# A decoder trunk on one core: two HGRN2 units' values and gates projected in one pass of 512 columns

## The chip, the cores and the metric

The kernel runs on one core of a Trainium2 chip. The core has a matrix engine (TensorE, PE in the profile; its weight loads are listed apart as PEld), a vector engine (VectorE, DVE), a scalar engine (ScalarE, ACT), a general engine (GpSimd, POOL) and a queue engine that issues transfers (SyncE, SP). They run side by side, each in its own order, and wait for one another by semaphores. TensorE writes its results into PSUM, here eight banks of 512 floats for each of 128 partitions; the other data stand in SBUF. The metric is device time in microseconds; less is better.

## The reference

One layer of a hybrid decoder for 2048 tokens of width 1024: a token mixer and a gated MLP, each behind a normalised, conditioned input and added to the residual.

```python
def token_mixer(h, w_in, w_gla_up, b_gla, lb, head_gain, w_out, pos):
    proj = h @ w_in
    (rq, rk, rv, rg, hq, hf, hi, hg, aq, ak, av, ag, alow) = jnp.split(proj, offs, axis=-1)
    ...
    z = split_heads(hf, HG_HEADS).astype(jnp.float32)
    log_f = jnp.logaddexp(jnp.log1p(-lbh) + jax.nn.log_sigmoid(z), jnp.log(lbh))
    key_h = (1.0 - lbh) * jax.nn.sigmoid(-z)
    o_h = gated_state_chunkwise(jax.nn.silu(split_heads(hq, HG_HEADS)), key_h,
                                split_heads(hi, HG_HEADS), log_f)
    o_h = merge_heads(rms_norm(o_h)) * jax.nn.silu(hg)
    ...
    o = jnp.concatenate([o_r, o_h.astype(o_r.dtype), o_a.astype(o_r.dtype)], axis=-1) * head_gain
    return o @ w_out
```

Three kinds of heads share the input projection: retention heads (r), HGRN2 heads (h) and gated linear attention heads (a). For the HGRN2 heads `hf` gives the forget gate and the key, `hq` the query, `hi` the values and `hg` the output gate, which acts as `hg * sigmoid(hg)` (a swish) on the normalised result.

## The kernel before

**Blocks and units.** The 2048 tokens are worked on in four blocks of 512 (`b` = 0 to 3), each in four chunks of 128. Within a block the mixer's heads form units of two heads each, 128 columns: four HGRN2 units `h0` to `h3`, one unit `g` that holds the two pairs of GLA heads, and two retention units `r0`, `r1`. The list `ORDER` runs them as h0, g, h1, h2, h3, r0, r1. After the mixer the MLP runs over all tokens from about 1274 us on; the change does not touch it.

**Precision.** Each product of float32 data is made of three matmuls (`split3`, L239): every operand is split into a rounded high part and the rest as low part, and high x high, high x low and low x high are added in PSUM. A weight piece comes as raw data by DMA, ScalarE casts the high part, VectorE subtracts to get the low part (`piece`, L217; in `tf512` L293 and L299), and the low part is stored in DRAM (`keep`), so that the later blocks load it instead.

**Projections.** `cf_gemm` (L251) gives one unit's f or q with channels on the partitions: 8 x 3 matmuls of 512 tokens. `tf_gemm` (L263) gives one unit's values and gates with tokens on the partitions: for each of 8 slices of the model width and each of four chunks three matmuls, the activations being the stationary operand and 256 weight columns (128 of values, 128 of gates) the moving one; two chunks share a bank. `tf512` (L281) does the same for two such pieces of 256 columns at once, one bank for each chunk, in four quarters of weights; before the change it is used for the two pairs of g and for the retention units (q, k beside v, g).

**Emptying the banks.** `tok_evac` (L517) after `tf_gemm` and `tok_evac4` (L526) after `tf512` bring values and gates to SBUF: ScalarE copies the values, ScalarE takes the sigmoid of the gates, VectorE multiplies that sigmoid with the gates, all three reading PSUM. `tok_evac4` does one unit's four banks, then the other's. Four banks (`acc_ps`) serve all large products in turn; two more are for the level steps (`lev_ps`) and two for the rest of the chains (`late_ps`).

**Chains.** A unit's recurrence (`gated`, L586; `retention`, L799) is a generator: some matmuls, then a pause in which VectorE and ScalarE work on them, and so on. A gated chain has seven level steps (L610 on TensorE; L618, L620, L629 on VectorE), then a transpose of the keys, the state update `u` (the first to read the values `v`), the output, and after a further pause the transposed result `oT`, which reads the gates.

**The order of TensorE's work is fixed when the program is built**, by a planner (`Clock`, L55). Every group of large matmuls advances a clock by its estimated time, and chain steps are issued into the stream when their pauses are over; `clock.until` issues what is due next until a condition holds. One chain runs at a time; the others stand in line. ScalarE, VectorE and the queues are put in order by the framework, by program order and given priorities.

**Around the units.** `out_half` (L908) is the output projection of a block, in two halves of four units: the first at the block's end, the second (`out_finish`, L927) in the next block behind h0, since it needs the last chains' results. It adds into the residual rows `x1`, which stand in four "xy" buffers, and forms the second norm; when the rows are done with (`then`, L935), the buffers come free. The same buffers serve `weight_sums` (L873), 22 small jobs that form sums of MLP weights on VectorE in blocks 1 to 3, and `early_sums` in block 3. `ada_next` brings in one row of the conditioning weights with each weight piece while any are queued, 16 of them in block 1; such a row uses one of the two raw weight buffers.

Of the kernel before, what the change touches and what calls it, by code (L numbers as in the profile page):

```python
# [9 lines left out]
F32 = mybir.dt.float32  # L10
# [3 lines left out]
AF = mybir.ActivationFunctionType  # L14
ALU = mybir.AluOpType
# [85 lines left out]
def trunk(ctx, tc, xT, vecs, cvec, cst, rope, msk, wada, win, walow, wgla, wout, wup, wdown, out):  # L101
# [24 lines left out]
    def late_ps(name):  # L126
        return pp.tile([P, 512], F32, tag="late", name=name, bufs=2)
# [152 lines left out]

    def tf512(name, i):  # L281

        pss = [acc_ps(f"ps{name}_{c}") for c in range(NCH)]
        for q4 in range(4):
            half, sub = q4 // 2, q4 % 2
            src = win[i + half:i + half + 3:2][:, :, sub * 512:(sub + 1) * 512].rearrange("a p n -> p a n")
            ada_next()
# [224 lines left out]
    def tok_tiles(name):  # L512

        return (pu.tile([P, NCH, P], F32, tag="v", name="v" + name, bufs=3),
                pu.tile([P, NCH, P], F32, tag="sg", name="sg" + name, bufs=3))

    def tok_evac(vsg, pss):  # L517
        v, sg = vsg
        for j, ps in enumerate(pss):
            p3 = ps[:].rearrange("p (c n) -> p c n", n=256)  # L520
            c2 = slice(2 * j, 2 * j + 2)
            S.copy(v[:, c2, :], p3[:, :, 0:P])
            S.activation(sg[:, c2, :], p3[:, :, P:256], AF.Sigmoid)
            V.tensor_tensor(sg[:, c2, :], sg[:, c2, :], p3[:, :, P:256], op=ALU.mult)

    def tok_evac4(vsg, pss, at):  # L526

        v, sg = vsg
        for c, ps in enumerate(pss):
            gate = ps[:, at + P:at + 256]  # L530
            S.copy(v[:, c, :], ps[:, at:at + P])
            S.activation(sg[:, c, :], gate, AF.Sigmoid)
            V.tensor_tensor(sg[:, c, :], sg[:, c, :], gate, op=ALU.mult)

# [51 lines left out]
    def gated(name, b, ui, pos, kq, decay, subs, qk, sel):  # L586
# [16 lines left out]
        for li, s in enumerate(LEVELS):  # L603
            nb = 64 // s
            pss = []
            for q, rows, v, sg in subs:
                ps = lev_ps(f"lv{name}_{s}")
                for c in range(NCH):
                    rhs = q[:, :, c * P:(c + 1) * P].rearrange("p h (n t s) -> p h n t s", t=2, s=s)[:, :, :, 1, :]
                    T.matmul(ps[:, c * P:(c + 1) * P].rearrange("p (h n s) -> p h n s", h=2, s=s),  # L610
                             kq[:, c * P:(c + 1) * P], rhs, start=True, stop=True)
                pss.append(ps)
            with tc.high_priority(offset=CHAIN):
                ev = tree[li]
                nn = TB // (2 * s)
                for q, rows, v, sg in subs:
                    qv = q[:].rearrange("p h (n t s) -> p h n t s", t=2, s=s)[:, :, :, 1, :]
                    V.tensor_tensor(qv, qv, ev[:, :, 0:1].unsqueeze(1).to_broadcast([P, 2, nn, s]), op=ALU.mult)  # L618
# [11 lines left out]
            adv(4 * len(subs) * MF)  # L630
            yield LEVEL_GAP[two]
        ps = late_ps("kT" + name)
        for c in range(NCH):
            T.transpose(ps[:, c * P:(c + 1) * P], kq[:, c * P:(c + 1) * P], ident)
        kT = pu.tile([P, NCH, P], F32, tag="kT", name="kT" + name, bufs=1)
        with tc.high_priority(offset=CHAIN):
            S.copy(kT[:].rearrange("p c n -> p (c n)"), ps[:])
            for q, rows, v, sg in subs:
# [4 lines left out]
        for q, rows, v, sg in subs:  # L643
            ps = late_ps("u" + name)
# [15 lines left out]
        os = []  # L660
        for i, ((q, rows, v, sg), at) in enumerate(zip(subs, attns)):
            if i:
# [20 lines left out]

    def unit_h(b, u, pos):
        nm = f"h{b}_{u}"
# [22 lines left out]
        clock.chain(gated(nm, b, u, pos, kq, decay, subs, qk, selh), 9.0 if b == u == 0 else 6.0)  # L708
        tok_evac(subs[0][2:], tf_gemm("vg" + nm, 4 * u + 2))

# [11 lines left out]
    def unit_g(b, pos):  # L722
# [38 lines left out]
        pss = tf512(f"vg{nm}", 18)  # L761
        for i in range(2):
            tok_evac4(subs[i][2:], pss, 256 * i)

    rots = {}

    def unit_r(b, r, pos):
# [11 lines left out]
        for c, ps in enumerate(pss):  # L779
            S.copy(a[0][:, c * P:(c + 1) * P], ps[:, 0:P])  # L780
            S.copy(a[1][:, c * P:(c + 1) * P], ps[:, P:256])
        tok_evac4(vsg, pss, 256)
        s4 = sin.unsqueeze(2).to_broadcast([P, NCH, 2, 32])
# [15 lines left out]
    def retention(nm, b, r, pos, a, kk, kc, q, vsg):  # L799
        v, sg = vsg  # L800
        Sst = states[5 + r]
# [226 lines left out]

    oTs = [[None] * KD for _ in range(NB)]
    mk = {"h": unit_h, "g": lambda b, u, pos: unit_g(b, pos), "r": unit_r}  # L1030
    PE, DVE, ACT, SP = (getattr(mybir.EngineType, n) for n in ("PE", "DVE", "Activation", "SP"))
    ctx.enter_context(tc.manual_schedule(engines={PE}))
# [3 lines left out]
    gla_weights()  # L1036
    for hi, lo, raw, i in W0.values():
        keep(f"i{i}l", lo[:])
    jobs = [job for k in range(NF // 2) for job in (("d", k), ("u", 2 * k + 1))]
    for b in range(NB):  # L1040
        pos = 0
# [522 lines left out]
```

## Time and profile before

| what | value |
|---|---|
| median of three runs | 2562.22 us |
| runs | 2557.1, 2562.22, 2563.71 us |
| the profiled execution's span | 2557.2 us |
| first matmul of the mixer's unit g in block 0 | 59.1 us |
| ends of the first output halves of blocks 0, 1, 2, 3 | 305.6, 617.1, 920.4, 1227.4 us |
| matmuls `psvgh<-hvgh,ha` etc. of 128x256 (values and gates of h units) | 1440 |
| matmuls `psqkvgr` and `psvgg` of 128x512 | 768 and 384 |

The device time of a run is about the span, so nothing noteworthy lies around it. In the profile a group of instructions is named by its line, engine, operation and out<-in, with buffer numbers and block numbers left out: `psvgh` is the bank of an h unit's values and gates, `psvgg` that of g, `pshfh` the bank of an h unit's f, `sgg` the gates of g in SBUF, `lvgh` the low part of a weight piece. Busy time of TensorE counts overlapping matmuls, so that its share says little; idle time and the distance between starts say more.

### The profile page before, as it was taken

Reading aid. Unit: us, or ns where it says so; the run is one execution under the profiler, and the core shown is the slowest. Engines: PE = TensorE matmul, PEld = TensorE weight load, DVE = VectorE, ACT = ScalarE, POOL = GpSimd, SP = SyncE. Lnnn points to the kernel's source line nnn. Section 1 sums busy time; section 2 is a strip of 40 time slices with the busy share of each in tenths; the row PEclk is TensorE's granted clock in tenths of the full one; section 3 lists DMA queues with packets and bytes.
Section 4 is the critical chain, followed back from the end, with each engine's and each line's share of the span. In section 5 each row is a group of like instructions: output and inputs, shape, how many; then the busy total and the mean of one; then the engine's idle time right before and its main releaser. Section 6 shows DMA issues by size and latency. Waiting matters only on the chain.

```text
span 2557.2 us, 37116 instructions
## 1 busy us (share of the span) xinstructions
PE 2493.1 (97%) x13146; PEld 2132.7 (83%) x13146; DVE 1973.8 (77%) x3596; ACT 1139.0 (45%) x1914; POOL 169.6 (7%) x303
## 2 busy tenths in 40 slices
PE   5999999999999999999899999999999999999998
PEld 4898888988889898898788888888878888888887
DVE  8788986878678776787688888887677778778666
ACT  4433434524444235333254555455444555455442
POOL 1000000000000000000200000000001001000000
PEclk9999999999999999999999999999999999999999
DMA  8454576775687847786745444477675544447663
GB/s 304 166 190 165 197 250 214 250 251 196 220 309 278 291 147 242 267 308 223 278 168 174 153 146 163 149 274 244 210 228 168 155 146 145 154 136 251 221 193 127
DMA packets 229337, 533.84 MB, mean 209 GB/s; under 512 B 25216, under 2 KB 28320, under 8 KB 229152
## 3 DMA queue, kind: packets, MB, share of 16 engines
q1 hardware_dynamic: 224672, 516.80, 59.5%
q0 software_dynamic: 4480, 14.68, 1.6%
q8 instruction: 103, 1.69, 0.3%
q14 instruction: 82, 0.67, 0.1%
HBM read 397.69 MB, written 133.69 MB: 208 GB/s over the span
## 4 chain that ended last, share of the span: by engine, by line
PE 78%; issue 9%; DVE 5%; DMA 4%; ACT 1%; SPq 0%; POOL 0%; DVEq 0%; ACTq 0%; POOLq 0%
PE X L241 6%; PE X L242 6%; PE X L243 6%; PE Z L241 3%; PE Z L242 3%; PE Z L243 3%; PE lvh L610 3%; PE y L241 2%; PE y L243 2%; PE y L242 2%; PE psqkvgr L243 2%; PE psqkvgr L241 2%; PE psqkvgr L242 2%; PE psvgh L242 2%; PE psvgh L241 2%
## 5 line engine op out<-in xcount | busy, mean ns | idle before, releaser
L241 PE MATMUL X<-B,A 128*128 128x512 f32 x572 | 223.5, 391 | 1.4 <-ACT u L1247 1.4
L242 PE MATMUL X<-B,A 128*128 128x512 f32 x572 | 222.9, 390 | 0.0
L243 PE MATMUL X<-B,A 128*128 128x512 f32 x572 | 222.9, 390 | 0.0
L974 DVE TENSOR_TENSOR dA<-rd,dA 128x512 fp32r<-128x512 f32 x154 | 106.1, 690 | 86.7 <-ACT dA L973 86.4
L973 ACT CAST dA<-rd 128x512 fp32r<-128x512 f32 x154 | 95.6, 621 | 139.9 <-PE dX L243 45.8
L974 DVE TENSOR_TENSOR A<-s,A 128x512 fp32r<-128x512 f32 x176 | 120.8, 686 | 43.7 <-ACT A L973 43.3
L973 ACT CAST A<-s 128x512 fp32r<-128x512 f32 x176 | 108.7, 618 | 71.5 <-PE Z L243 45.2
L241 PE MATMUL psvgh<-hvgh,ha 128*128 128x256 f32 x480 | 140.0, 292 | 0.0
L241 PE MATMUL dX<-dB,dA 128*128 128x512 f32 x352 | 137.1, 390 | 0.0
L243 PE MATMUL dX<-dB,dA 128*128 128x512 f32 x352 | 137.1, 390 | 0.0
L242 PE MATMUL dX<-dB,dA 128*128 128x512 f32 x352 | 137.1, 390 | 0.0
L242 PE MATMUL psvgh<-lvgh,ha 128*128 128x256 f32 x480 | 135.9, 283 | 1.1 <-DVE lvgh L233 1.1
L243 PE MATMUL psvgh<-hvgh,ha 128*128 128x256 f32 x480 | 135.9, 283 | 0.0
L241 PEld LDWEIGHTS X<-B,A 128*128 128x128 f32 x572 | 107.5, 188 | 24.3 <-ACT u L1247 2.2
L243 PEld LDWEIGHTS X<-B,A 128*128 128x128 f32 x572 | 107.5, 188 | 22.1
L242 PEld LDWEIGHTS X<-B,A 128*128 128x128 f32 x572 | 107.5, 188 | 22.1
L610 PEld LDWEIGHTS lvh<-qbh,kh 128*128 128x128 f32 x896 | 115.2, 191 | 8.8 <-issue 1.0
L610 PE MATMUL lvh<-qbh,kh 128*128 128x128 f32 x896 | 120.1, 277 | 1.1 <-DVE kh L620 1.0
L241 PE MATMUL Z<-B,A 128*128 128x512 f32 x308 | 120.6, 392 | 0.0
L242 PE MATMUL Z<-B,A 128*128 128x512 f32 x308 | 120.5, 391 | 0.0
L243 PE MATMUL Z<-B,A 128*128 128x512 f32 x308 | 120.4, 391 | 0.0
L974 DVE TENSOR_TENSOR dB<-rb,dB 128x512 fp32r<-128x512 f32 x154 | 105.7, 687 | 13.2 <-ACT dB L973 13.1
(463 smaller groups left out, 7129.8 us busy)
## 6 DMA issues: line engine op xcount, KB each, us to landing
gs<-yv SPq DMA_DIRECT2D x154, 256.0 KB, 2.8
rb<-gs SPq DMA_DIRECT2D x154, 256.0 KB, 4.0
r<-wup SPq DMA_DIRECT2D x141, 256.0 KB, 3.3
s<-sumsu SPq DMA_DIRECT2D x132, 256.0 KB, 3.0
wada<-wada SPq DMA_DIRECT2D x48, 512.0 KB, 5.1
rd<-sumsd SPq DMA_DIRECT2D x88, 256.0 KB, 3.8
rd<-wdown SPq DMA_DIRECT2D x66, 256.0 KB, 3.8
x<-xT SPq DMA_DIRECT2D x64, 256.0 KB, 5.6
```

What stands on the lines that cost most here:

```text
L241: T.matmul(ps, lhs[0], rhs[0], start=first, stop=False, skip_group_check=more)
L242: T.matmul(ps, lhs[0], rhs[1], start=False, stop=False, skip_group_check=more)
L243: T.matmul(ps, lhs[1], rhs[0], start=False, stop=last, skip_group_check=more)
L610: T.matmul(ps[:, c * P:(c + 1) * P].rearrange("p (h n s) -> p h n s", h=2, s=s), kq[:, c * P:(c + 1) * P], rhs, start=True, stop=True)
L973: S.copy(hi, src)
L974: V.tensor_tensor(lo, src, hi, op=ALU.subtract)
```

## The change

Two HGRN2 units' values and gates are now projected by one `tf512` pass, in place of one `tf_gemm` each. `tf512` gets a step, so that it can take the weight pieces of units 2k and 2k+1, which lie four apart. The first unit of a pair only makes its f and q and hands its tiles on; the second makes its own f and q and then the pass for both. This is done for units 2 and 3 of block 0 and for all units of blocks 1 to 3; units 0 and 1 of block 0 stay single.

Values and gates of a unit now share one tile of 256 columns per chunk. A bank is emptied by one copy per unit (128x256 each in a wide pass, 128x512 after `tf_gemm`), bank after bank and both units in each; the sigmoid and the product of the gates are done afterwards from SBUF, over all four chunks in one instruction each. A unit counts as landed when these instructions have been issued, and a gated chain waits in the planner before its transpose of the keys until its unit has landed.

In blocks 1 to 3 the units run as h0, h1, g, h2, h3, r0, r1, and the second half of the previous block's output projection follows h1 in place of h0. The low parts of units 0's values and gates, made at the start, are no longer stored.

```diff
-    def tf512(name, i):
+    def tf512(name, i, step=2):
...
-            src = win[i + half:i + half + 3:2][:, :, sub * 512:(sub + 1) * 512].rearrange("a p n -> p a n")
+            src = win[i + half:i + half + step + 1:step][:, :, sub * 512:(sub + 1) * 512].rearrange("a p n -> p a n")
...
     def tok_tiles(name):
 
-        return (pu.tile([P, NCH, P], F32, tag="v", name="v" + name, bufs=3),
-                pu.tile([P, NCH, P], F32, tag="sg", name="sg" + name, bufs=3))
-
-    def tok_evac(vsg, pss):
-        v, sg = vsg
+        t = pu.tile([P, NCH, 256], F32, tag="v", name="v" + name, bufs=3)
+        return t[:, :, 0:P], t[:, :, P:256], (t, name)
+
+    landed = set()
+
+    def swish(name, sg):
+
+        t = tmp("sw" + name)[:].rearrange("p (c n) -> p c n", n=P)
+        S.activation(t, sg, AF.Sigmoid)
+        V.tensor_tensor(sg, sg, t, op=ALU.mult)
+
+    def tok_evac(name, vsg, pss):
+        v, sg, both = vsg
         for j, ps in enumerate(pss):
-            p3 = ps[:].rearrange("p (c n) -> p c n", n=256)
-            c2 = slice(2 * j, 2 * j + 2)
-            S.copy(v[:, c2, :], p3[:, :, 0:P])
-            S.activation(sg[:, c2, :], p3[:, :, P:256], AF.Sigmoid)
-            V.tensor_tensor(sg[:, c2, :], sg[:, c2, :], p3[:, :, P:256], op=ALU.mult)
-
-    def tok_evac4(vsg, pss, at):
-
-        v, sg = vsg
+            S.copy(both[0][:, 2 * j:2 * j + 2, :], ps[:].rearrange("p (c n) -> p c n", n=256))
+        swish(name, sg)
+        landed.add(both[1])
+
+    def tok_evac4(name, units, pss):
+
         for c, ps in enumerate(pss):
-            gate = ps[:, at + P:at + 256]
-            S.copy(v[:, c, :], ps[:, at:at + P])
-            S.activation(sg[:, c, :], gate, AF.Sigmoid)
-            V.tensor_tensor(sg[:, c, :], sg[:, c, :], gate, op=ALU.mult)
+            for at, (v, sg, both) in units:
+                S.copy(both[0][:, c, :], ps[:, at:at + 256])
+        for at, (v, sg, both) in units:
+            swish(f"{name}{at}", sg)
+            landed.add(both[1])
...
+        while any(sub[-1][1] not in landed for sub in subs):
+            yield 1.5
         ps = late_ps("kT" + name)
...
-    def unit_h(b, u, pos):
+    def unit_h(b, u, pos, then=None):
...
-        tok_evac(subs[0][2:], tf_gemm("vg" + nm, 4 * u + 2))
+        if then is None:
+            tok_evac(nm, subs[0][2:], tf_gemm("vg" + nm, 4 * u + 2))
+            return
+        other = then(subs[0][2:])
+        if other is not None:
+            tok_evac4(nm, [(0, other), (256, subs[0][2:])], tf512("vg" + nm, 4 * u - 2, 4))
...
-        for i in range(2):
-            tok_evac4(subs[i][2:], pss, 256 * i)
+        tok_evac4(nm, [(256 * i, subs[i][2:]) for i in range(2)], pss)
...
-        tok_evac4(vsg, pss, 256)
+        tok_evac4(nm, [(256, vsg)], pss)
...
+    held = []
+
+    def first_of_two(vsg):
+        held.append(vsg)
+
+    def second_of_two(vsg):
+        return held.pop()
...
-    for hi, lo, raw, i in W0.values():
+    for hi, lo, raw, i in (W0["f"], W0["q"]):
         keep(f"i{i}l", lo[:])
...
-        for i, (kind, u) in enumerate(ORDER):
+        for i in range(len(ORDER)) if b == 0 else (0, 2, 1, 3, 4, 5, 6):
+            kind, u = ORDER[i]
+            pos = i + (i > 1)
             if i == len(ORDER) - 3 and b + 1 < NB:
                 norm1_stat(b + 1)
-            mk[kind](b, u, pos)
-            pos += 2 if kind == "g" else 1
+            if kind == "h" and (b or u > 1):
+                unit_h(b, u, pos, second_of_two if u % 2 else first_of_two)
+            else:
+                mk[kind](b, u, pos)
...
-            if i == 0 and b:
+            if i == 2 and b:
                 clock.until(lambda: None not in oTs[b - 1])
                 out_finish(b - 1)
```

More of the change, by code (lines that the diff above doesn't have):

```diff
@@ L605, in gated @@
             pss = []
-            for q, rows, v, sg in subs:
+            for q, rows, v, sg, _ in subs:
                 ps = lev_ps(f"lv{name}_{s}")
@@ L615, in gated @@
                 nn = TB // (2 * s)
-                for q, rows, v, sg in subs:
+                for q, rows, v, sg, _ in subs:
                     qv = q[:].rearrange("p h (n t s) -> p h n t s", t=2, s=s)[:, :, :, 1, :]
@@ L637, in gated @@
             S.copy(kT[:].rearrange("p c n -> p (c n)"), ps[:])
-            for q, rows, v, sg in subs:
+            for q, rows, v, sg, _ in subs:
                 r0, r1 = rows[1]
@@ L642, in gated @@
         yield 1.8
-        for q, rows, v, sg in subs:
+        for q, rows, v, sg, _ in subs:
             ps = late_ps("u" + name)
@@ L660, in gated @@
         os = []
-        for i, ((q, rows, v, sg), at) in enumerate(zip(subs, attns)):
+        for i, ((q, rows, v, sg, _), at) in enumerate(zip(subs, attns)):
             if i:
@@ L799, in retention @@
     def retention(nm, b, r, pos, a, kk, kc, q, vsg):
-        v, sg = vsg
+        v, sg, _ = vsg
         Sst = states[5 + r]
@@ L1040, in trunk @@
     for b in range(NB):
-        pos = 0
         if b == 2:
             later += range(40, 48)
-        for i, (kind, u) in enumerate(ORDER):
+        for i in range(len(ORDER)) if b == 0 else (0, 2, 1, 3, 4, 5, 6):
+            kind, u = ORDER[i]
+            pos = i + (i > 1)
             if i == len(ORDER) - 3 and b + 1 < NB:
                 norm1_stat(b + 1)
-            mk[kind](b, u, pos)
-            pos += 2 if kind == "g" else 1
+            if kind == "h" and (b or u > 1):
+                unit_h(b, u, pos, second_of_two if u % 2 else first_of_two)
+            else:
+                mk[kind](b, u, pos)
             if b == 0 and i == 2:
```

## The prediction

> **What bounds the kernel now.** I read the page first, then the table of stages, then TensorE's waits, then single stretches of the timeline.
>
> ```profile
> span 2557.2 us, 37116 instructions
> PE 2493.1 (97%) x13146; PEld 2132.7 (83%) x13146; DVE 1973.8 (77%) x3596; ACT 1139.0 (45%) x1914; POOL 169.6 (7%) x303
> PE 78%; issue 9%; DVE 5%; DMA 4%; ACT 1%; SPq 0%; POOL 0%; DVEq 0%; ACTq 0%; POOLq 0%
> ```
>
> ```profile
> 59.00:305.00 246.00, 243.83 (x1516) 215.44 (x1517) 201.82 (x448) 98.55 (x191) 9.61 (x17) 1.00 0.53 185
> 305.00:617.00 312.00, 309.01 (x1921) 274.07 (x1920) 245.89 (x576) 129.92 (x235) 17.51 (x30) 1.00 0.66 227
> 617.00:920.00 303.00, 301.44 (x1871) 267.12 (x1870) 236.39 (x551) 120.04 (x221) 15.78 (x26) 1.00 0.75 261
> 920.00:1227.00 307.00, 302.37 (x1856) 267.52 (x1855) 224.36 (x511) 120.01 (x227) 18.24 (x30) 0.99 0.69 244
> 1227.00:1274.00 47.00, 37.82 (x181) 31.06 (x180) 27.42 (x52) 13.66 (x25) 11.91 (x25) 0.96 0.83 303
> ```
>
> The first four stages are the mixer's blocks 0 to 3 (columns: length, then busy time of PE, PEld, DVE, ACT, POOL, then clock, DMA share, GB/s). TensorE is idle for 1.6 to 4.6 us in each: a block lasts as long as its matmuls take to issue, plus a few stalls. VectorE, at 73 to 82%, is the second engine. All work of the change lies before 1227 us. The waits of TensorE name the stalls:
>
> ```profile
> PE ssn L319 <- DVE san L340: 6.0, 1, 6.0
> PE pshfh L241 <- ACT sgg L532: 4.1, 1, 4.1
> PE psvgh L242 <- DVE lvgh L233: 1.1, 1, 1.1
> ```
>
> So the change can win in two ways, cheaper issue of the same products or a stall removed, and lose in one, a new stall.
>
> **Cheaper issue.** A matmul's duration in the trace overlaps the next one's, so the price of one is the distance of starts.
>
> ```profile
> 325.68 0.28 PE L241 MATMUL psvgh<-hvgh,ha 128*128 128x256 f32 x1
> ...
> 332.03 0.28 PE L243 MATMUL psvgh<-hvgh,ha 128*128 128x256 f32 x1
> ...
> 1018.79 0.39 PE L242 MATMUL psvgg<-lvgg,ha 128*128 128x512 f32 x1
> ...
> 1020.38 0.39 PE L243 MATMUL psvgg<-hvgg,ha 128*128 128x512 f32 x1
> ```
>
> The first pair of rows are the 1st and 54th matmul of an unbroken stretch of 256 columns: 6.35/53 = 0.1198 us each. The second pair are the 1st and 8th of a stretch of 512 columns, of just the form that the new passes have: 1.59/7 = 0.2271. One unit's values and gates are 8 slices x 4 chunks x 3 = 96 matmuls of 256 columns. A pair of units costs 192 x 0.1198 = 23.0 us now and 96 x 0.2271 = 21.8 after: **1.2 us less per pair**. There are 7 pairs (units 2 and 3 of block 0; both pairs of blocks 1 to 3): **-8.4 us**. Nothing lies beside this on TensorE, it is the path itself. Bounds: -7.4 (0.120 against 0.229, as in passes that are often broken by level steps) to -10.
>
> The Trainium skill (TensorE: Matmul & The Clock Gate, "Wait — 56ns, not 53.3ns?") puts the cost that a warm matmul has beyond its columns at about 2.5 ns; the rows put it at 2 x 119.8 - 227.1 = 12.5 ns. By the page, 7 x 96 x 2.5 ns is an estimated 1.7 us instead of 8.4: it is taken up as a rival.
>
> **The emptying of banks.** Now L522 to L524 and L531 to L533 read each bank three times, the last time on VectorE; after, ScalarE copies and the rest works in SBUF.
>
> ```profile
> L522 ACT COPY vh<-psvgh 128x256 f32<-128x256 f32 x32 | 11.9, 373 | 50.2 <-PE psvgh L243 50.1
> L523 ACT ACTIVATE sgh<-psvgh 128x256 f32<-128x256 f32 x32 | 12.5, 393 | 0.1
> L524 DVE TENSOR_TENSOR sgh<-sgh,psvgh 128x256 f32<-128x256 f32 x32 | 13.3, 417 | 10.1 <-ACT sgh L523 9.8
> L691 ACT ACTIVATE sfh<-pshfh 128x512 f32<-128x512 f32 x15 | 8.8, 588 | 1.4 <-PE pshfh L243 1.4
> L703 DVE TENSOR_TENSOR sqh<-sqh,fh 128x512 f32<-128x512 f32 x16 | 11.0, 688 | 0.1
> ```
>
> Two units cost ScalarE 4 x (0.373 + 0.393) = 3.1 us now, and 8 x 0.373 + 2 x 0.588 = 4.2 after; VectorE 4 x 0.417 = 1.7 now, 2 x 0.688 = 1.4 after. With ScalarE under 45% busy the extra microsecond is hidden. What matters is when a bank comes free: two copies, 0.75 us, against the 6 x 0.227 = 1.36 us that TensorE spends on a bank in the pass's last quarter. So ScalarE follows bank by bank, and only if it is held for over 4 us (three banks' work) does the next product wait. I take 0, bounds 0 and +1 per block.
>
> For the gated unit g the order of release matters today: unit 0's gates of all four banks are worked off before unit 1's first copy, so bank 0 comes free after the last. In block 3 this went wrong:
>
> ```profile
> 1024.27 0.40 PE L243 MATMUL psvgg<-hvgg,ha 128*128 128x512 f32 x1
> 1028.73 0.77 PE L241 MATMUL pshfh<-ha,hhfh 128*128 128x512 f32 x1 [4.05 <-ACT sgg L532]
> ...
> 1033.98 0.54 PE L241 MATMUL pshfh<-ha,hhfh 128*128 128x512 f32 x1
> 1028.22 0.27 ACT L531 COPY vg<-psvgg 128x128 f32<-128x128 f32 x1 [2.13 <-DVE sgg L533]
> 1025.05 2.43 DVE L629 COPY_PREDICATED atg<-m_all,lvg 128x512 f32<-128x512 uint32 x2
> ```
>
> TensorE idled 4.05 us because ScalarE's copy waited for VectorE's gate product in the same bank, which stood behind 2.43 us of level masks. The stall costs more than its length: the next twelve matmuls start (1033.98 - 1028.73)/12 = 0.4375 us apart, at about half speed, 12 x 0.21 = 2.5 us more. From 1024.27 the first full-speed start would be 0.23 later, so the whole is 4.2 + 2.5 = **6.7 us**. After, no VectorE instruction reads these banks and both units leave bank 0 first. I take -6.7; bounds -6.7 and 0 (ScalarE itself may be late).
>
> **The extra low parts.** Units 0 and 1 of block 0 keep the old weight layout, so block 1 has no stored low parts for its first pair: four subtractions on VectorE and four stores in place of four loads. Block 0 makes as many as before. Two stores of units 0's low parts go. Raw loads stay four per pair.
>
> ```profile
> L299 DVE TENSOR_TENSOR lqkvgr<-rqkvgr,hqkvgr 128x1024 fp32r<-128x1024 f32 x8 | 9.8, 1225 | 3.8 <-ACT hqkvgr L293 3.8
> L197 DVE CUSTOM_DVE_ANT_0 wada<-wada,c_act,vec 128x1024 f32<-128x1024 f32 x32 | 40.9, 1281 | 9.7 <-DMA wada<-wada 8.7 <-issue 0.8
> 320.00:330.00 10.00, 10.00 (x77) 9.48 (x76) 9.68 (x24) 2.76 (x4) 1.60 (x3) 1.00 0.51 191
> 330.00:340.00 10.00, 10.00 (x88) 10.00 (x87) 9.55 (x21) 3.79 (x7) 0.00 (x0) 1.00 0.78 279
> 340.00:350.00 10.00, 10.00 (x56) 8.60 (x55) 9.38 (x15) 3.91 (x6) 0.00 (x0) 1.00 0.66 231
> ```
>
> 4 x 1.225 = 4.9 us fall where VectorE is 94 to 97% busy, and in the same passes each piece also brings a conditioning row (1.28 us), which shares the two raw buffers. Hidden if that stretch has slack, all exposed if not: +2 taken, bounds 0 and +5 (plus 2.5 of slow clock should one wait pass 4 us).
>
> **The order.** In blocks 1 to 3 unit 1 moves ahead of g, and the last half of the previous block's output projection now stands behind units 0 and 1 instead of behind unit 0: 48 matmuls of f and q and 96 wide ones come before it, 96 narrow ones leave: 48 x 0.227 + 21.8 - 11.5 = 21 us, with the level steps that fall inside about 24. Unit 0's chain waits in the planner until its values land, but it gives its 7 level steps during unit 1's products, which last longer; TensorE is not empty meanwhile: 0, with +1 as bound. Queued behind the late projection are its rows x1. They hold all four "xy" buffers, for which the weight sums of block 2 wait, and for those the next x1 rows:
>
> ```profile
> 690.15 0.33 SPq L877 DMA_DIRECT2D wsd<-wdown  x1
> 868.40 0.69 DVE L884 TENSOR_TENSOR wsu<-wsu,wsu 128x512 f32<-128x512 f32 x1
> 863.64 0.38 SPq L916 DMA_DIRECT2D x<-xT  x1
> 877.56 0.85 SPq L916 DMA_DIRECT2D x<-xT  x2
> DMA to landing us min/median/max: 3.5/6.3/7.5
> 887.65 0.75 DVE L920 SCALAR_TENSOR_TENSOR x<-y,mod,x 128x512 f32<-128x512 f32 x1
> 901.62 0.74 DVE L920 SCALAR_TENSOR_TENSOR x<-y,mod,x 128x512 f32<-128x512 f32 x1
> ```
>
> The 12 jobs run back to back from 690 to 869, and the rows are issued at 864 to 878 for a use at 888. Shifted by 24 the first row lands at 864 + 6 + 24 = 894 and is used at about 888 - 5 = 883 (the block's own gain): 11 us late. But four banks stand between: the fifth row block takes the first bank only near 902 - 5 = 897. So the slack falls to about 3 us. I take +1, bounds 0 and +8 here; the price beyond that is the slower rival.
>
> At the mixer's end the order brings the last chain some microseconds earlier against the products, so the stretch 1227 to 1274 may lose a little of its idle 9 us: -1 taken, bounds -8 and +4.
>
> **Sum:** -8.4 - 6.7 + 2 + 1 - 1 = -13.1 on a profiled 2557.2, hence 2544. That execution lies at the low end of the runs shown (2557.1 to 2563.7, the span fills it), 5.0 under their median, so the median goes to 2562.2 - 13.1 = **2549**.
>
> **Rivals.** A measurement of this kernel can tell 0.3%, 7.7 us, from no change.
>
> (a) *Only the narrow saving.* ScalarE is held itself when g's banks are full (casts of the sums made early, masks, weight casts), or a like stall comes elsewhere: -8.4 + 2 + 1 - 1 = -6.4, 2556. For it: the stall came once in four blocks, so it hangs on chance order; against: the released instruction waited for VectorE, which is out of the way.
>
> (b) *The fixed cost is 2.5 ns:* 7 x 96 x 2.5 ns = 1.7 in place of 8.4, so -6.4 again, 2556. The rows of both widths speak against it. This is the page's rule, named above.
>
> (c) *VectorE becomes the bound in block 1:* two quarters of the new pass each wait over 4 us at 6.7 a time: -13.1 - 2 + 13.4 = -1.7, 2560. For it 94 to 97%; against: TensorE has no idle time there now.
>
> (d) *The x1 rows come too late, slower.* Place: end of block 2. If each of the 12 jobs also takes 2 us longer, rows come 24 us later still, 21 beyond the cover, and the slow clock adds 2.5: -13.1 - 1 + 23.5 = +9.4, 2572. It decides from a slip of about 3 us beyond the 24. For it: the chain of jobs has no gaps; against: the same work, no more bytes, and in block 3 the rows are in time by over 20 us.
>
> (e) *The end of the mixer tightens too:* its 8 us go: -13.1 - 7 = -20, 2542.
>
> **Chances.** Forecast 0.50, (a) 0.16, (b) 0.04, (c) 0.08, (d) 0.12, (e) 0.10. Faster by over 7.7 us (under 2554.5): nearly all of the forecast, (e), some of (a): 0.63. Within: 0.24. Slower: 0.13. The range 2541 to 2564 holds (e) to (c) with the run's spread and leaves out (d) and tails.
>
> **What would show it.** Starts of 0.227 us in the units' passes and 7 x 96 wide in place of 14 x 96 narrow matmuls; no wait of pshfh for sgg, and no half-speed stretch behind g in block 3; VectorE over 95% in block 1's first 60 us, with waits for the new low parts if that step is too small; x<-xT of block 2 issued near 888. Wrong it would be by a new idle stretch of TensorE over 4 us in blocks 1 to 3, or by a narrow pass that proves as cheap per column as a wide one.

## The result, and the profile after

The changed kernel takes **2585.48 us** (median of four runs, 2583.08 to 2588.48) beside 2562.97 us of the kernel before on the same chip (2557.1 to 2564.02): ratio 1.01, 95% interval 1.0088 to 1.0112. (The medians by themselves lie 22.5 us apart, 0.88%; below, differences in time go by the ratios.) The kernel is slower, and its time lies above the 2541 to 2564 us forecast. These are the first lines of the page of after, with the busy times and the chain that ended last.

```profile
span 2586.7 us, 35564 instructions
PE 2492.4 (96%) x12474; PEld 2100.2 (81%) x12474; DVE 1969.1 (76%) x3536; ACT 1153.3 (45%) x1878; POOL 169.2 (7%) x303
PE 78%; DVE 11%; DMA 7%; ACT 2%; issue 2%; SPq 0%; DVEq 0%; ACTq 0%
```

There are 672 matmuls fewer, which is 7 x 96 as planned, and TensorE is still on 78% of the chain. VectorE and transfers have grown on it, from 5 and 4% to 11 and 7%; a part of that lies ahead of and behind the four blocks, where the time hardly differs. The table of stages says where the time went (blocks 0 to 3; columns as in the prediction):

```profile
60.00:314.00 254.00, 246.48 (x1423) 213.44 (x1424) 198.73 (x428) 102.19 (x178) 9.54 (x16) 0.99 0.51 174
314.00:642.00 328.00, 313.57 (x1757) 269.47 (x1756) 254.41 (x576) 133.82 (x229) 20.08 (x34) 0.98 0.62 216
642.00:958.00 316.00, 301.15 (x1678) 257.83 (x1677) 234.65 (x534) 122.85 (x213) 15.90 (x27) 0.98 0.72 250
958.00:1261.00 303.00, 299.17 (x1664) 256.58 (x1663) 219.69 (x492) 124.22 (x220) 15.29 (x26) 0.99 0.70 247
```

Blocks 0, 1 and 2 are 7, 16 and 13 us longer than before, and TensorE idles 7.5, 14.4 and 14.9 us in them where it idled 2.2, 3.0 and 1.6. Block 3 is 4 us shorter. After the mixer little differs: 1294.9 us before, 1293.0 after. TensorE's waits name the new stalls (us in total, times, longest):

```profile
PE psvgh L241 <- ACT hvgh L293: 10.0, 1, 10.0
PE psvgh L241 <- ACT snh L700: 6.8, 1, 6.8
PE bcn L329 <- DVE rsn L158: 4.1, 3, 3.0
PE oTh L558 <- DVE oh L552: 3.2, 1, 3.2
PE y L243 <- DVE lwo L233: 2.8, 1, 2.8
```

The two largest stand at the wide pass of units 2 and 3: in block 2 ahead of its first product, in block 1 behind its first 12. Block 2 first. This is SyncE's queue before it (start, duration, line, transfer); TensorE is idle from 806.6 on.

```profile
791.24 0.43 SPq L484 DMA_DIRECT2D x<-xT  x1
793.01 0.33 SPq L889 DMA_DIRECT2D wsu<-wup  x1
797.02 0.33 SPq L898 DMA_DIRECT2D sumsd<-wsd  x1
797.43 1.20 SPq L484 DMA_DIRECT2D x<-xT  x2
800.36 0.33 SPq L890 DMA_DIRECT2D wsu<-wup  x1
800.96 0.33 SPq L899 DMA_DIRECT2D sumsd<-wsd  x1
801.38 2.89 SPq L484 DMA_DIRECT2D x<-xT  x4
807.19 0.33 SPq L898 DMA_DIRECT2D sumsu<-wsu  x1
808.52 0.33 SPq L899 DMA_DIRECT2D sumsu<-wsu  x1
808.94 0.40 SPq L484 DMA_DIRECT2D x<-xT  x1
809.39 0.73 SPq L290 DMA_DIRECT2D rvgh<-win  x1
```

L484 is `norm1_stat`, the statistics of the **next** block's first norm: eight loads of rows, their squares and sums, and a short chain of its own. The wide pass's first raw weights (L290) are issued only behind the eighth row, at 809.39, almost 3 us after TensorE ran dry. Between the rows stand the stores of the weight sums (L898), which wait for VectorE; in the waits of SyncE's queue from 770 to 820 us they are the first and the third:

```profile
SPq L898 <- DVE wsd L894: 9.5, 2, 5.9
SPq L290 <- DMA rvgh<-win: 7.0, 3, 3.3
SPq L898 <- DVE wsu L894: 6.2, 2, 3.3
```

Before, the same eight rows came at another point of the block: behind the level steps of g's chain, whose transpose `kTg` follows the last level. Here are both, first of before and then of after (transpose from TensorE's timeline, rows from SyncE's; block 2).

```profile
759.92 0.60 PE L634 MATMUL kTg<-c_all,kg 128*128 128x128 f32 x4
767.38 7.27 SPq L484 DMA_DIRECT2D x<-xT  x5
```

```profile
829.04 0.60 PE L642 MATMUL kTg<-c_all,kg 128*128 128x128 f32 x4
```

Before, the first row is issued 7 us after the transpose; after, 38 us ahead of it, in the midst of g's levels. The reason is in the loop: `norm1_stat` is tied to `i == len(ORDER) - 3`, ahead of h3, and h1 and g have changed places. So the statistics meet g's chain, two units' f and q and one large pass at once.

Block 1's stall is the same in another place. TensorE waits until ScalarE has read the bank of h3's f (`sfh`, `snh`). ScalarE's timeline:

```profile
497.25 0.63 ACT L336 ACTIVATE san<-x 128x512 f32<-128x512 f32 x1 [2.22 <-DMA x<-xT]
...
500.79 1.15 ACT L339 ACTIVATE sqn<-x 128x512 f32<-128x512 f32 x2
502.17 0.63 ACT L339 ACTIVATE sqn<-x 128x512 f32<-128x512 f32 x1 [0.24 <-DVE san L340]
502.71 0.58 ACT L699 ACTIVATE sfh<-pshfh 128x512 f32<-128x512 f32 x1
503.19 1.21 ACT L339 ACTIVATE sqn<-x 128x512 f32<-128x512 f32 x2
504.30 0.58 ACT L700 ACTIVATE snh<-pshfh 128x512 f32<-128x512 f32 x1
```

The two reads of the bank, 0.6 us each, stand among the statistics' squares (L336, L339), and the squares wait for rows. The stall lasts from 498.2 to 504.9.

Block 3 has no next block and so no statistics. There the stall behind g is gone: the first product of h2 follows g's last at full pace.

```profile
1092.46 0.39 PE L243 MATMUL psvgg<-hvgg,ha 128*128 128x512 f32 x1
1092.68 0.39 PE L241 MATMUL pshfh<-ha,hhfh 128*128 128x512 f32 x1
```

### The profile page after: what moved, and what is told of

It is laid out like the page before. It is cut to its first block, busy times and chain, and to the rows that moved or that the text cites. A ratio compares the mean times of both kernels' runs of the same rounds, so it can differ in the third digit from the quotient of the medians.

```text
span 2586.7 us, 35564 instructions
## 1 busy us (share of the span) xinstructions
PE 2492.4 (96%) x12474; PEld 2100.2 (81%) x12474; DVE 1969.1 (76%) x3536; ACT 1153.3 (45%) x1878; POOL 169.2 (7%) x303
## 3 DMA queue, kind: packets, MB, share of 16 engines
q0 software_dynamic: 4480, 14.68, 1.6%
## 4 chain that ended last, share of the span: by engine, by line
PE 78%; DVE 11%; DMA 7%; ACT 2%; issue 2%; SPq 0%; DVEq 0%; ACTq 0%
PE X L241 6%; PE X L242 6%; PE X L243 6%; PE lvh L616 4%; PE Z L242 3%; PE Z L241 3%; PE Z L243 3%; PE dX L242 3%; PE dX L243 3%; PE dX L241 3%; PE psqkvgr L243 2%; PE psqkvgr L241 2%; PE psqkvgr L242 2%; PE psvgh L241 2%; PE psvgh L242 2%; PE psvgh L243 2%
## 5 line engine op out<-in xcount | busy, mean ns | idle before, releaser
L241 PE MATMUL psvgh<-hvgh,ha 128*128 128x512 f32 (+1 forms) x256 | 103.2, 403 | 16.8 <-ACT hvgh L293 10.0
L986 DVE TENSOR_TENSOR A<-r,A 128x512 fp32r<-128x512 f32 x130 | 89.2, 687 | 29.8 <-ACT A L985 29.7
L985 ACT CAST A<-r 128x512 fp32r<-128x512 f32 x130 | 80.8, 623 | 62.5 <-PE Z L243 59.2
```

Source lines behind the costliest of these rows:

```text
L241: T.matmul(ps, lhs[0], rhs[0], start=first, stop=False, skip_group_check=more)
L985: S.copy(hi, src)
L986: V.tensor_tensor(lo, src, hi, op=ALU.subtract)
```

## The experiments

All runs in one table: median, ratio to the kernel before on the same chip with its interval, and in the profiled execution the lengths of blocks 0 to 3 (block 0 from the first matmul of its unit g, each block to the start of the large product that follows its first output half).

| kernel | us | ratio (95%) | block 0 | 1 | 2 | 3 |
|---|---|---|---|---|---|---|
| before | 2562.97 | 1 | 246.5 | 311.5 | 303.3 | 306.9 |
| after | 2585.48 | 1.01 (1.0088 to 1.0112) | 253.8 | 327.7 | 316.6 | 302.9 |
| e1 later statistics | 2566.33 | 1.0025 (1.0014 to 1.0035) | 256.2 | 314.6 | 303.4 | 300.4 |
| e2 narrow pair | 2599.88 | 1.0156 (1.014 to 1.0173) | 252.9 | 331.3 | 325.5 | 301.2 |
| e3 before, statistics earlier | 2564.19 | 1.0019 (1.0009 to 1.0029) | 247.2 | 316.3 | 303.8 | 305.4 |
| e4 before, new emptying | 2566.38 | 1.0022 (1.001 to 1.0034) | 250.5 | 317.7 | 304.9 | 299.6 |
| f1 rows in other buffers | 2581.67 | 1.0071 (1.0056 to 1.0086) | 249.4 | 320.1 | 321.8 | 303.6 |
| f2 e1, gates bank by bank | 2567.93 | 1.0021 (1.0012 to 1.003) | 255.4 | 319.0 | 303.4 | 301.1 |
| f3 e1, stored low parts | 2571.7 | 1.0033 (1.0023 to 1.0043) | 255.7 | 319.1 | 303.5 | 302.4 |
| f4 e4, gates bank by bank | 2557.47 | 0.9979 (0.997 to 0.9989) | 250.4 | 311.5 | 305.5 | 299.6 |
| g1 e1, narrow pair | 2578.33 | 1.0067 (1.005 to 1.0084) | 257.8 | 320.4 | 310.3 | 303.1 |
| g2 raw loads first | 2600.15 | 1.0149 (1.0134 to 1.0164) | 258.2 | 331.9 | 323.3 | 298.9 |
| g3 f1 and g2 | 2587.47 | 1.0101 (1.0078 to 1.0124) | 250.2 | 325.2 | 327.4 | 298.6 |
| g4 f4, block 0 emptied as before | 2556.25 | 0.9974 (0.9961 to 0.9988) | 248.0 | 311.2 | 303.7 | 300.7 |
| h1 rows on another queue | 2583.03 | 1.0081 (1.0066 to 1.0096) | 253.4 | 333.4 | 307.7 | 300.9 |
| h2 other queue and buffers | 2568.07 | 1.0023 (1.0013 to 1.0033) | 250.4 | 317.6 | 305.1 | 301.2 |
| h3 pairs from block 1 on | 2556.72 | 0.9982 (0.9973 to 0.9991) | 248.4 | 318.0 | 302.6 | 300.1 |

**e1: the statistics later.**

```diff
-            if i == len(ORDER) - 3 and b + 1 < NB:
+            if i == len(ORDER) - 2 and b + 1 < NB:
```

> The changed kernel (2585 us) with the statistics of the next block's first norm (norm1_stat) one unit later, before r0 instead of before h3. Theory S (the statistics, tied to the unit's number, now fall into g's chain and take temporaries and queue places that the paired units need): the stalls of blocks 1 and 2 at the wide pass (6.9 and 10.2 us) and the waits for the broadcast (3.2, 1.4, 2.5) go, 20 to 35 us less: 2550 to 2565. Theory W (the wide pass needs all four banks at once and so waits for the banks of f and q): nothing or under 5 us, 2580 to 2585. Theory V (VectorE is overfull through the later gate work and the new low parts): under 8 us, 2577 to 2585.

One number in the loop takes back 19 us, just under the 20 to 35 that theory S had, and far more than the two others. The two large stalls are gone and blocks 1 and 2 fall by 13 us each. Block 2's rows now come behind g's chain again:

```profile
807.78 0.60 PE L642 MATMUL kTg<-c_all,kg 128*128 128x128 f32 x4
833.87 6.94 SPq L484 DMA_DIRECT2D x<-xT  x8
```

In block 0 the later statistics do harm: they meet h1's outputs, and its transpose waits longer (PE waits, e1):

```profile
PE oTh L558 <- DVE oh L552: 9.2, 3, 5.7
```

**e2: the same order, two narrow passes in place of the wide one.**

```diff
-            tok_evac4(nm, [(0, other), (256, subs[0][2:])], tf512("vg" + nm, 4 * u - 2, 4))
+            tok_evac(nm + "a", other, tf_gemm(f"vgh{b}_{u - 1}", 4 * u - 2))
+            tok_evac(nm, subs[0][2:], tf_gemm("vg" + nm, 4 * u + 2))
```

> The changed kernel, but the pair's values and gates come from two narrow passes, one after the other, at the place of the wide one; order of units, evacuation by copies and place of the statistics as changed. By the issue price alone it is 8.4 us slower than the changed kernel. Theory S: the collision stays, 2580 to 2600. Theory W: with two banks for each pass the stalls behind f and q go (about 20 us), 2565 to 2575. Theory V: as S.

Stalls of the same size stay, at other instructions. In block 1 the bank is no longer waited for, but 36 products of values and gates later TensorE waits 7.3 us for the statistics' own sum (`ssn` for `san`). In block 2 it waits 10.8 us for the low part of h3's q. So the cost doesn't come from the pass's width, or from its need of four banks at once. By width the kernel gains 1.56 - 1.0 = 0.56%, 14 us.

**e3: the kernel before, with the statistics ahead of h2 instead of h3.**

```diff
-            if i == len(ORDER) - 3 and b + 1 < NB:
+            if i == len(ORDER) - 4 and b + 1 < NB:
```

> The kernel before with the statistics of the next block's first norm one unit earlier (before h2 instead of before h3), so that they fall into g's chain as they do in the changed kernel; nothing paired. Theory S: slower by 10 to 30 us, 2572 to 2592. Theories W and V: within 4 us of before, 2559 to 2567.

A miss for theory S: it costs 0.2%, 4.9 us, all in block 1, and lies where theories W and V had it, which e1 and e2 speak against. In block 2 its rows come 20 us ahead of g's transpose (745.6 against 765.1), and the block is as long as before. Early statistics alone do little in the old order; that they hurt in the new one, through the pair's weights and banks, is left for f1, h1 and h2 to show.

**e4 and f4: the emptying alone.** Both are after with the loop of before (its order, single narrow passes), so that of the change the new emptying is left; f4 also works on each bank's gates as soon as they are copied. The first lines are of both, those behind the second mark of a gap of f4.

```diff
-        for i in range(len(ORDER)) if b == 0 else (0, 2, 1, 3, 4, 5, 6):
+        for i in range(len(ORDER)):
...
-            if kind == "h" and (b or u > 1):
-                unit_h(b, u, pos, second_of_two if u % 2 else first_of_two)
-            else:
-                mk[kind](b, u, pos)
+            mk[kind](b, u, pos)
...
         for j, ps in enumerate(pss):
-            S.copy(both[0][:, 2 * j:2 * j + 2, :], ps[:].rearrange("p (c n) -> p c n", n=256))
-        swish(name, sg)
+            c = slice(2 * j, 2 * j + 2)
+            S.copy(both[0][:, c, :], ps[:].rearrange("p (c n) -> p c n", n=256))
+            swish(t, sg, c)
```

> The kernel before with only the new emptying of the banks (one tile for values and gates, copies by ScalarE, sigmoid and product afterwards from SBUF); narrow passes, order and place of the statistics as before. Theory S: the stall behind g in block 3 goes (4.2 + 2.5 us) and little else changes, 2554 to 2562. Theory V: slower, 2566 to 2575. Theory W: 2556 to 2564.

> The kernel before with the new emptying of banks (2566 us in the lumped form), gates bank by bank from SBUF. Theory L: the new waits of blocks 0 and 1 (3.3 and 4.0 us) go and block 3 keeps its gain of 7, 2552 to 2559. Rival (the shared tile or the later release is at fault, not the lump): 2563 to 2569.

In both, block 3 takes 299.6 us, 7.3 less than before, and the wait of `pshfh` for `sgg` is gone. TensorE's idle time there goes from 4.63 to 0.27 us (stage of f4's block 3):

```profile
926.00:1226.00 300.00, 299.73 (x1858) 265.72 (x1857) 224.16 (x513) 125.05 (x227) 18.27 (x30) 1.00 0.72 250
```

e4 gives this back in blocks 0 and 1 (+4.0 and +6.2), so that its total misses the 2554 to 2562 expected: its gates stand as one lump over four chunks on ScalarE and VectorE. Bank by bank block 1 returns to 311.5, and the whole is faster than before.

**f1: the statistics' rows in the other group of buffers** (those of the attention tiles), so that they don't take the slots of the temporaries.

```diff
-            x = tmp(f"x{b}_{k}")
-            nc.sync.dma_start(x[:], xT[b, :, k, :])
+            x = pa.tile([P, D], F32, tag="a4k", name=f"x{b}_{k}")[:, 0:TB]
+            nc.sync.dma_start(x, xT[b, :, k, :])
```

> The changed kernel (2585 us), statistics in their old place before h3, but their eight input rows go through tiles of the a4k ring instead of the ring of six temporaries that the units' sigmoids and products use. Theory S-ring (the rows and the temporaries of two waiting units shut each other out: the row loads block the queue of transfers and f's bank is emptied late): the 6.9 us stall of block 1 and the 10.2 us stall of block 2 go, 2562 to 2572. Theory S-time (the statistics' instructions on VectorE and ScalarE collide with g's chain, whatever tiles they use): under 6 us gained, 2578 to 2586.

Block 1's stall is gone (320.1), block 2's is not (321.8); it has only moved to other weights, and the total lies where the rival, S-time, had it:

```profile
PE pshqh L241 <- ACT hhqh L229: 5.9, 1, 5.9
PE psvgh L242 <- DMA lvgh<-keptt_0l: 4.6, 1, 4.6
```

**f2 and f3: what is left in e1.** f2 is e1 with the gates bank by bank, as in f4. f3 is e1 with block 1's new low parts left out: it loads g's stored ones in their place.

```diff
+        if b == 1:
+            kept.update({f"t2_{n}l": kept[f"t18_{n}l"] for n in range(4)})
```

> The kernel with later statistics (2566 us), and the gates worked on bank by bank: after the copies of a bank its sigmoid and product follow at once, from SBUF (128 columns each), instead of all four chunks at the end. Theory L (the gate work in one lump at the end of a pass leaves VectorE idle during the pass and overfull in the level steps behind it, so that low parts and the chain's last results come late): the 3.3 us wait before h0's transposed result in block 0 and part of the others go, 2555 to 2562. Rival: VectorE's order there hangs on something else, 2564 to 2570 (more instructions).

> The kernel with later statistics (2566 us), but block 1's first pair takes stored low parts: those of g's weights are loaded in their place, so that the four subtractions and four stores of block 1 are left out and the products of that pair get wrong low parts. If the extra low parts cost what was forecast: the wait for the output weights' low part in block 1 (3.2 us) goes, 2 to 5 us less, 2561 to 2564. If block 1's VectorE is late for other reasons: under 1.5 us less.

Neither gains (+5.4 and +8.5 us over before by the ratios, e1 +6.4). So the extra low parts cost nothing that can be seen.

**g1: e1 with narrow pairs.** The edit is e1's and e2's together.

> The kernel with the later statistics (2566.3 us), but each pair of units projected by two narrow passes of 256 columns one after the other, in the place of the one wide pass. If the wide pass's cheaper starts (7 pairs x 1.2 us = 8.4 us by the start-to-start durations) reach the end of the kernel, this one takes 2572 to 2578 us. If something else takes them back (a wait that moves), it takes 2563 to 2569 us.

It is 0.42% slower than e1: the width is worth 10.8 us here, 8.4 within the spread.

**g2 and g3: the raw loads of the wide passes first.** With the loads the edit also raises their casts and low parts. g3 has f1's buffers too.

```diff
     def tf512(name, i, step=2):
...
-            with tc.high_priority(offset=50):
+            with tc.high_priority(offset=400):
```

> The changed kernel with the wide passes' raw weight loads, their casts and low parts given a higher priority (400 in place of 50), so that on SyncE's queue they stand ahead of the statistics' rows; TensorE's order is the same. Theory Q (the queue): block 2's wait of 10.2 us for the first cast weights of the wide pass is gone, block 2 falls from 316.6 to 304 to 309 us, block 1's wait of 6.9 us at its wide pass (temporaries' slots) stays, in all 2573 to 2579 us. Rival T (the statistics' own work on ScalarE and VectorE inside the chains, whatever the order of the loads): 2581 to 2589 us, and block 2 above 313 us with the wait moved to another instruction.

> Both at once: the wide passes' raw loads first, and the statistics' rows in the other group of buffers (2581.7 us by itself). If queue and slots together make up the cost of the early statistics, this comes down to what the later statistics gave, 2562 to 2570 us, with blocks 1 and 2 near 315 and 304 us. If the statistics' own work in the chains is the cost, it stays at 2576 to 2584 us.

Both missed; g2 is worse than after by 0.5%. In g2 block 2's first raw load is issued at 792.74 instead of 809.39, but now TensorE stalls earlier, and longer, in the pass of q (PE waits of g2; the second line is block 1's):

```profile
PE pshqh L243 <- DMA lhqh<-kepti12l: 15.8, 1, 15.8
PE psvgh L241 <- ACT snh L700: 8.3, 1, 8.3
```

The low part of q was issued at 817.46, behind rows and stores that waited. To take one load out of the line only makes another the last. So the order in the queue is not the cure, but this alone doesn't tell the queue from the statistics' work.

**h1 and h2: the rows off SyncE's queue.** h1 is after with the rows issued by GpSimd; h2 has f1's buffers too. Everything else stays, TensorE's order and the place of the statistics among it.

```diff
-            nc.sync.dma_start(x[:], xT[b, :, k, :])
+            nc.gpsimd.dma_start(x[:], xT[b, :, k, :])
```

> The changed kernel with the eight row loads of each block's statistics issued from GpSimd's queue instead of SyncE's; everything else, TensorE's order too, as it was. Theory Q2 (SyncE's one queue: loads stand behind the weight sums' stores, which wait for VectorE, and each row ahead of them makes the last one late): block 2's wait of 10.2 us is gone, block 2 near 305 to 309 us, block 1's 6.9 us at the wide pass (slots) may stay, in all 2570 to 2579 us. Rival T (the statistics' squares and sums inside the chains, whatever queue loads them): block 2 stays above 313 us, in all 2581 to 2590 us. GpSimd also clears the attention tiles; if a row that waits for its slot holds those up, a new wait at the tiles' clearing shows it.

> The same with the rows in the other group of buffers as well (2581.7 us with that alone). If queue and slots are the two costs, both waits are gone: 2561 to 2570 us, as with the later statistics (2566.3 us). If the statistics' own work is the cost: 2576 to 2584 us.

h1 cures block 2 (307.7), as the theory had it, and spoils block 1 (333.4), so that its total misses the 2570 to 2579 expected and lies where the rival's was. In block 1 a row waits on GpSimd's queue for a slot, and TensorE for the bank as before, only longer (waits of h1, 478 to 515 us):

```profile
POOL x L484 <- ACT t L953: 53.5, 1, 53.5
PE psvgh L241 <- ACT snh L700: 12.4, 1, 12.4
```

The slot was held by temporaries of the second norm (`t`, L953). h2 takes queue and slots away: both stalls are gone, the whole takes 2568.07, and the largest of TensorE's waits for the units' weights that is left behind the start-up is

```profile
PE psvgh L242 <- DMA lvgh<-keptt_2l: 2.0, 1, 2.0
```

The statistics still come ahead of the end of g's levels, earlier even than in after, as less holds them up:

```profile
736.18 2.12 POOL L484 DMA_DIRECT2D x<-xT  x4
...
805.36 0.60 PE L642 MATMUL kTg<-c_all,kg 128*128 128x128 f32 x4
```

So early statistics as such are not the cost; that their rows come late and in the way is, through queue and slots: 1.01 - 1.0023 = 0.77%, some 20 us. f1 and h1 alone give only 7 and 5 of it, since each leaves the other wait. The squares move with the rows: in block 2 ScalarE does them from 749.7 to 767.5 in h2 and from 797.4 to 814.9 in after. Whether they would also cost something if they fell just on the pair's passes, with their rows in time, was not tried.

Between h2 and f1 only the issuing engine differs, and with it the transfer queue that carries the rows (`software_dynamic`, 6400 packets instead of 4480): 1.0071 - 1.0023, 12 us. The Trainium skill (DMA: Bandwidth & Descriptors, "Issuing engines are not separate DMA queues") says that another issuing engine saves only the time to issue, usually little. Here it saved more. The waits of SyncE's queue above suggest why: what stood in line were not only issues but stores that waited for VectorE. A run that keeps the transfer queue and moves only the place in line was not made.

**g4 and h3: can the parts be put together?** g4 is f4 with the old emptying straight from the banks in block 0. h3 is e1 from block 1 on; in block 0 it has no pairs, the old emptying, and the statistics at their old place. These are h3's lines against e1, without those of the emptying.

```diff
-            if i == len(ORDER) - 2 and b + 1 < NB:
+            if i == len(ORDER) - (2 if b else 3) and b + 1 < NB:
...
-            if kind == "h" and (b or u > 1):
+            if kind == "h" and b:
```

> The kernel of before with the new emptying whose gates are worked on bank by bank (2557.5 us, block 0 250.4 us against 246.5 us before), but in block 0 the old emptying straight from the banks. If the new emptying costs block 0 its 3 to 4 us (the wait of 3.3 us ahead of the first transposes of h0's output at 121 us), block 0 comes back to 246 to 248 us, the others stay, and the whole takes 2552 to 2555 us. If the wait has another source (the tiles that hold values and gates together), block 0 stays at 250 us and the whole takes 2556 to 2559 us.

> The parts put together that were best by themselves: block 0 without pairs, with the old emptying and the statistics where they were (248.0 us in the kernel that had the old emptying in block 0 alone); blocks 1 to 3 with wide passes, the new emptying and the later statistics (314.6, 303.4 and 300.4 us there). The sum is 59.3 + 248.0 + 314.6 + 303.4 + 300.4 + 33.8 + 1293 = 2552.5 us of span: 2549 to 2556 us if the parts add up, which would be the fastest of all and would show that the wide pass pays from block 1 on. If a part of it comes back elsewhere (low parts that block 1 now forms itself, with VectorE busy there), 2557 to 2563 us.

g4 brings block 0 from 250.4 to 248.0, and its wait of 3.0 us for h0's output becomes 0.7 (PE waits, 100 to 140 us, f4 and then g4):

```profile
PE oTh L564 <- DVE oh L558: 3.0, 1, 3.0
```

```profile
PE oTh L582 <- DVE oh L576: 0.7, 1, 0.7
```

As a whole g4 can't be told from f4, and at 2556.25 us it misses the 2552 to 2555 expected by a little; both beat before and after. h3 is faster than before too, but no faster than f4 or g4, which have no pairs at all. At 2556.72 us it lies just between the 2549 to 2556 expected if the parts add up and the 2557 to 2563 if not: of its blocks, 2 and 3 are together 2.4 us shorter than f4's and 1.7 than g4's; block 1 is 6.5 and 6.8 longer than theirs. Summed by the distances of starts, 3.1 us of that are work moved there from the end of the mixer (24 products of the retention units' outputs and a transpose); for the rest block 1 shows short waits in the second half of the output projection (2.6 us for `lwo`, 1.8 for an h unit's output). They were not taken apart.

## Why the prediction was wrong

**In steps.** By the ratios, with a thousandth as 2.56 us, the way from before to after is: new emptying +5.6 (e4); units grouped in pairs, still narrow and with the statistics put later, +11.5 (g1); widened -10.8 (e1); statistics where the change has them +19.2 (after). In all +25.6 by after's own ratio (the steps are rounded), where -13.1 was forecast. Each ratio's interval is 1 to 2 thousandths to either side, so a step is known to some 3 to 5 us.

**Cheaper issue, -8.4: right.** Starts of 128x512 in the units' passes lie 0.227 us apart (median). Summed by the distances of their starts, the values and gates of the four units take 47.0 us in block 1 of g4 and 44.9 in that of h3: 2.1 where 2.4 were forecast for two pairs, hence some 7.4 for seven, at the forecast's lower bound. In whole runs the width gave 10.8 and 14 us. So rival (b), with 1.7, falls.

**The stall behind g, -6.7: right.** Block 3 loses 7.3 us in e4 and in f4. In the changed kernel it loses only 4.0 where 7.3 and 2.4 of issue should add up; of the 5.7 that are missing 2.7 went into one wait for a stored low part in its second pair's pass, which 3.41 us at half the clock follow.

**The emptying at 0, bounds 0 and +1 per block: too low.** The sum looked at when banks come free, which was right, and not at when the gates are finished. Gates of four chunks in a lump cost 4.0 us in block 0 and 6.2 in block 1 (e4). Done bank by bank, block 1's cost goes; in block 0 2.4 us belong to the new emptying, by g4, in whatever form.

**The order at 0 to +1: this step failed.** It listed what is queued behind the late output projection and found the x1 rows, which came in time (VectorE never waits for one): rival (d) had the direction right and the mechanism wrong. What was left out is that a piece of work in the loop hangs on the **index** of a unit, not on the state of the chains. With g behind h1 the end of g's levels slid from 7 us ahead of the statistics' first row to 38 us behind it (block 2). The rows then stand in SyncE's queue among stores that wait for VectorE, ahead of the pair's weights, and in the slots of the temporaries, with ScalarE's reads of a bank behind their squares. e1 shows the place, f1, h1 and h2 the two resources. A second part of this step is that grouping by itself costs: with narrow passes and later statistics 11.5 us (g1 against e4), which takes back all that the width gives. This includes the later statistics' harm in block 0, which is 7.3 us longer in g1 than in e4; what makes up the rest stays open.

**The extra low parts, +2: nothing seen** (f3). Rival (c) falls with it. **The mixer's end, -1:** the stretch behind block 3's first half went from 35.0 to 32.6 us, of which 3.1 is work moved away, so nothing was gained.

**What would show it wrong** was named, a new idle stretch of over 4 us in blocks 1 to 3, and there are two, of 6.8 and 10.0. What a wait costs beyond its length was put at 2.5 us, and only above 4 us; the last section shows that shorter waits are followed by slow products too.

## What to carry to other kernels

When units of a loop change places, list everything that the loop does at a fixed index, loads for the next block above all, and put each beside the chain that it will now meet. A saving of issue time is easily worked out and easily lost: here 1.2 us per pair is a tenth of one late weight load. And where a load is late, ask of queue and buffer separately: each alone cured one stall and left or deepened the other; it took both to bring the time back with the loads in their early place.

## What was not expected of the hardware

After a wait the products run at half speed for a while, and the length of it isn't fixed. After the 10.0 us in block 2:

```profile
816.60 0.80 PE L241 MATMUL psvgh<-hvgh,ha 128*128 128x512 f32 x1 [10.01 <-ACT hvgh L293]
817.20 0.63 PE L242 MATMUL psvgh<-lvgh,ha 128*128 128x512 f32 x1
...
818.90 0.63 PE L243 MATMUL psvgh<-hvgh,ha 128*128 128x512 f32 x1
819.33 0.50 PE L241 MATMUL psvgh<-hvgh,ha 128*128 128x512 f32 x1
819.67 0.40 PE L242 MATMUL psvgh<-lvgh,ha 128*128 128x512 f32 x1
```

From 817.20 to 818.90 the starts lie 0.425 us apart, and by 819.67, 3.1 us after the wait, the pace is full. The shorter wait before the change (4.05 us) was followed by twelve slow starts, 5.3 us. The granted clock in the traces explains both: it is 0.5 from 809.31 to 819.55 in the one case, 10.24 us, and from 1027.46 to 1034.29 in the other, 6.83 us. These are three and two times 3.41 us, and so it is in every kept trace: all changes of the clock lie whole multiples of 3.41 us apart, and the stretches at half clock between them last one to six such steps. So the slow time behind a wait hangs on where the wait falls on this grid, and not on its length alone. Waits far below 4 us can set it off: in after those of 3.2, 3.0, 2.8 and 2.7 us (at 123.0, 194.1, 395.7 and 1138.0) each have one step at half clock behind them, while in h2 one of 2.8 us (at 393.8) has none. Blocks 0 to 3 of after spend 30.7 us at half clock, those of before 6.8. TensorE runs for 20.3 and 5.6 us of that; half of it is lost, so the slow clock makes up an estimated 7 us of what the change costs.

The Trainium skill (TensorE: Matmul & The Clock Gate, "What's actually happening") has a window of about 3.4 us that runs freely and decides on the clock; the grid of 3.41 us agrees with that. Its 426.7 ns from start to start at half clock for 512 columns ("Wait — 56ns, not 53.3ns?") agrees with the rows, its 2.5 ns beyond the columns at full clock doesn't (12.5 by the prediction's rows).
